# One block for the four upper levels of a recurrence's score matrix, and four residual sums moved to accumulating transfers

## The chip, the cores and the metric

The program runs on one core of one Trainium2 chip. The metric is the device time of one launch in microseconds (us). The kernel before takes 2004.77 us, the median of three runs that lie between 2004.34 and 2007.78 us.

## What is computed

A network of two layers on 1024 tokens of width 1024, all in float32: layer 0 mixes tokens by a sliding-window attention, layer 1 by a gated recurrence of eight heads, and each layer ends with an MLP. The change touches the recurrence alone. Cut to that:

```
def chunk_step(state, inp):            # one chunk of 64 tokens, all heads
    qc, kc, vc, lc = inp               # lc: log of the forget gate
    b = cumsum(lc, axis=2)
    o_inter = einsum('bhtd,bhde->bhte', qc * exp(b), state)
    diff = b[:, :, :, None, :] - b[:, :, None, :, :]
    decay = exp(where(causal, diff, -inf))
    scores = einsum('bhtd,bhtsd,bhsd->bhts', qc, decay, kc)
    o_intra = einsum('bhts,bhse->bhte', scores, vc)
    new_state = exp(b_last) * state + einsum('bhsd,bhse->bhde', kc * exp(b_last - b), vc)
    return new_state, o_inter + o_intra
...
o = rmsnorm(o, g_norm) * silu(g)
x = x + o @ w_o                        # the residual sum after the projection
```

## The kernel before, in words

Activations lie transposed, 128 channels on the partitions and 512 tokens (one half, `hf`) on the free axis. Every large product is a Strassen scheme of matmuls of 128x128 on 512 columns, each made of three (`wh` times high part, `wh` times low part, `wl` times high part), so that a row of three such matmuls is the unit in which TensorE's work is seen.

`Schedule` sets the order. Every operation is recorded with the engines that may run it and a planned cost; a list scheduler runs through them several times, hands out buffers, and writes each engine's instructions in the order that it found. Nothing is reordered on the chip: each engine, and SyncE's queue of transfers, takes its instructions in that order, and waits where an operand is late. All operations are issued by one helper line, so that every row of the profile carries L438; buffers are told apart by their pool: `p` and `q` are PSUM banks (four each), `t` (18 buffers), `a` (60) and `m` (6) are tiles of 128x512 in SBUF, `wr`, `wh` and `wl` hold weights, `d` is DRAM.

In `recurrence`, one call for each head `e`, the decayed scores inside a chunk are found by levels. At each level `double(H, ...)` multiplies half of the elements of `q` and half of those of `k` by the running products of forget gates (`tot`), and matmuls on 32 columns of the array (16 to 64 columns of data each) form the scores between neighbouring blocks of H tokens. `double` works in place, or, with a third argument such as `self.t`, writes new tiles from that pool: then the untouched half is copied by ScalarE. A group of such narrow matmuls is a visit (`visit`): it takes one bank of `q`, and each matmul of the group is made to wait for all operands of the group (`late`), so that the group stands in one piece between the wide matmuls. Before the change a head has four visits: level 0 (64 matmuls of 48 columns), levels 1 and 2 (128 of 16), levels 3 and 4 (128 of 16), and the two upper levels, 5 and 6 (32 of 32 columns and 32 of 64). `merge` copies the scores of a level into the tile `scores` under a mask on VectorE. The gates of the next head, wide matmuls, are laid between the pieces of a head's recurrence (`interleave`); the last head has the first products of the projection beside it.

`hgrn_out` is that projection, seven products in the order 1, 5, 2, 6, 3, 7, 4. After each of the last ones `scaled_sum(hf, m, z)` scales four PSUM banks on VectorE, loads the old residual, and adds. What comes out of the last product, 4, is `x[4..7][0]`; `begin` of the second MLP scales these (`gained`, ScalarE), splits them into high and low parts (ScalarE, then VectorE), and `pair_first` multiplies them into the banks that its rows call `p`. `dma_add` is a transfer issued by GpSimd that adds its source to its destination; it stands in other places of the kernel already.

Of the kernel before, what the change touches and what calls it, by code (L numbers as in the profile page):

```python
# [15 lines left out]
ALU = mybir.AluOpType  # L16
# [137 lines left out]
HK = KT // 2  # L154
# [229 lines left out]
class Net:  # L384
# [1347 lines left out]
    def recurrence(self, e, gates, totals, out):  # L1732
# [5 lines left out]
        tots, tot = [self.t(tag="m") for _ in range(NH)], [g[1] for g in gates]  # L1738
        qs, ks = ([g[i] for g in gates] for i in (0, 2))
        later = lambda z, H: z.rearrange("p (n a h) -> p n a h", a=2, h=H)[:, :, 1]  # L1740
        at = 0

        def level(lg, bank, at, qs, ks, late):
            n = NC * QB // 2
            part = bank[:, at * n : at * n + n].rearrange("p (c t) -> p c t", c=NC)
            for hf, (q, k) in enumerate(zip(qs, ks)):
                for j in range(4 * BPH):
                    rows = slice(j % 4 * QB, j % 4 * QB + QB)
                    self.mm(part[rows, hf * BPH + j // 4], block(k, j), later(block(q, j), 1 << lg), True, True, QB, 1.28, "columns", late)
            return part  # L1750

        def merge(lg, part):
            H = 1 << lg
            n = QB // (2 * H)
            mask = later(self.level_mask[lg], H).unsqueeze(1).to_broadcast([P, NC, n, H])
            target = scores.rearrange("p c (n a h) -> p c n a h", a=2, h=H)[:, :, :, 1]
            part = part if lg == 0 else part.rearrange("p c (n h) -> p c n h", n=n)
            self.op("DVE", nc.vector.copy_predicated, [target], [mask, part], 70 + NC * QB // 2 * 1.04, target, mask, part)

        def visit(operands):  # L1760
            return sum((q + k for q, k in operands), []), self.psum("q")

        for q, f, k, g, v in gates:
            for z, c in zip(q, PAIR):
                z = self.fours(z)
                self.tt("any", z[:, :, ::3].only("f"), z[:, :, 1:3].only("q"), self.pairs(f[:, c]), ALU.mult, TH // 2)
        yield
        late, bank = visit([(sum(qs, []), ks)])
# [10 lines left out]
        at, tot, q1, k1 = self.first_double(qs, ks, tot, tots)  # L1779
        yield  # L1780
        yield
        at, tot, q2, k2 = self.second_double(q1, k1, tot, tots, at)
        yield
        late, bank = visit([(sum(q1, []), k1), (q2, k2)])
# [7 lines left out]
        parts = [part, level(2, bank, 1, q2, k2, late)]  # L1792
        merge(1, parts[0])
        merge(2, parts[1])
        at, tot, qs, ks = self.double(4, q2, k2, tot, tots, at)
        yield
        yield
        at, tot, q4, k4 = self.double(8, qs, ks, tot, tots, at, self.t)
        yield
        late, bank = visit([(qs, ks), (q4, k4)])  # L1800
        parts = [level(3, bank, 0, qs, ks, late), level(4, bank, 1, q4, k4, late)]
        merge(3, parts[0])
        merge(4, parts[1])
        at, tot, q5, k5 = self.double(16, q4, k4, tot, tots, at)
        yield
        yield
        at, tot, q6, k6 = self.double(32, q5, k5, tot, tots, at, self.t)
        yield
        late, bank = visit([(q5, k5), (q6, k6)])
        top = bank[:, : NC * QB // 2].rearrange("p (c t) -> p c t", t=QB)  # L1810
        cross = bank[:, TH // 2 :].rearrange("p (c t) -> p c t", t=CH)
        for hf, (q, k) in enumerate(zip(q5, k5)):
# [3 lines left out]
        for hf, (q, k) in enumerate(zip(q6, k6)):  # L1816
            for j in range(2 * BPH):
                c, r = j // 2, (j // 2 % 2 * 2 + j % 2) * QB
                self.mm(cross[r : r + QB, (hf * BPH + c) // 2], block(k, 4 * c + j % 2), block(q, 4 * c + 2, 2), True, True, CH, 1.05,
                        "columns", late)  # L1820
        qs, ks = q6, k6
        yield
        weights = []
# [12 lines left out]
        at, tot, qs, ks = self.double(CH, qs, ks, tot, tots, at)  # L1836
# [4 lines left out]
        for hf, (q, k) in enumerate(zip(qs, ks)):  # L1841
            v, g = back[2 * hf : 2 * hf + 2]
# [149 lines left out]
    def hgrn_out(self, x, totals):  # L1992

        kept, y, r = {}, {}, [self.a() for _ in range(NH)]
        order = [(name, p) for name in ORDER for p in range(HK)]
        ready = {}

        def operand(name, p):
            w = self.out_weight(name, p, kept)
            z = x[name][p]  # L2000
            return w, self.take_back(z) if isinstance(z, list) else z

        def products(name, bank, start, apart=False):
            todo = order.index((name, 0))
            for p in range(HK):
                for q in order[: todo + p + 1 + AHEAD]:
                    if q not in ready:
                        ready[q] = operand(*q)
            got = [ready[name, p] for p in range(HK)]
            turns = [(p, m) for p in range(HK) for m in range(HK)]  # L2010
            more = {} if start else {"skip_group_check": True}
            for p, m in sorted(turns, key=lambda k: k[1]) if apart else turns:
                c, (w, z) = slice(m * P, m * P + P), got[p]
                self.mm3(bank[m], (w[0][:, c], w[1][:, c]), z, start and p == 0, p == HK - 1, **more)

        def scaled_sum(hf, m, z):
            u, out = self.t(tag="m"), self.a()
            self.tt("DVE", u, z, r[hf], ALU.mult)
            self.dma(out, self.x[m][hf], 4 * P * TH)
            self.tt("any", out, u, out, ALU.add)  # L2020
            self.x[m][hf] = out

        for hf in range(NH):
            self.copy(r[hf], self.rstd(totals[hf], 0.25, 0.25))
        main, side = [self.psum() for _ in range(HK)], [self.psum("q") for _ in range(HK)]
        p1, p5 = ([self.a() for _ in range(HK)] for _ in range(2))
        products(1, main, True)
        for m in range(HK):
            self.copy(p1[m], main[m])
        products(5, main, False)  # L2030
        for m in range(HK):
            w, z = ready[2, 0]
            self.mm(side[m], w[0][:, :P], z[0], True, True)
            self.copy(side[m], p1[m], psum=False)
            self.tt("DVE", p5[m], main[m], p1[m], ALU.subtract)
        products(2, side, False)
        for m in range(HK):
            scaled_sum(0, m, side[m])
        yield
        products(6, main, False)  # L2040
        for m in range(HK):
            self.copy(side[m], main[m])
        products(3, side, False)
        for m in range(HK):
            scaled_sum(1, m, side[m])
        products(7, main, False)
        for m in range(HK):
            self.tt("DVE", side[m], main[m], p5[m], ALU.subtract)
            scaled_sum(1, m + HK, main[m])
        products(4, side, False)  # L2050
        for m in range(HK):
            scaled_sum(0, m + HK, side[m])
        yield
# [153 lines left out]
```

## Time and profile before

| what | value |
|---|---|
| median of the runs | 2004.77 us |
| the profiled execution: its time | 2005.34 us |
| its span, first to last instruction | 2003.4 us |
| TensorE busy | 1992.5 us (99%) |
| VectorE busy | 1810.6 us (90%) |
| ScalarE busy | 1314.1 us (66%) |
| GpSimd busy | 88.3 us (4%) |
| granted TensorE clock, mean | 0.999 |

The time of the profiled execution is 1.9 us longer than its span, and 0.57 us above the median of the three runs. The eight heads lie between about 946 and 1325 us of the span, the projection ends at about 1385 us, and the second MLP follows without a break.

### The profile page before, as it was taken

How to read it: one execution, taken by the hardware profiler on the slowest of the kernel's cores; microseconds unless marked ns; L12 is line 12 of the kernel's file. 1: busy time of each engine (PE TensorE's matmuls, PEld its weight loads, DVE VectorE, ACT ScalarE, POOL GpSimd, SP SyncE). 2: the span in 40 equal slices, each digit the busy share in tenths (PEclk: the TensorE clock that was granted, in tenths of full speed). 3: DMA queues.
4: the chain of work that ended last, by engine and by line, in shares of the span. 5: the costliest groups of instructions: out<-in, count | busy, mean ns of one | idle time of the engine just before them, and what ended most of it. 6: DMA issues, size and time to landing. Idle time of an engine off the chain costs nothing.

```text
span 2003.4 us, 40001 instructions
## 1 busy us (share of the span) xinstructions
PE 1992.5 (99%) x13772; PEld 1692.1 (84%) x13772; DVE 1810.6 (90%) x3669; ACT 1314.1 (66%) x2783; POOL 88.3 (4%) x163
## 2 busy tenths in 40 slices
PE   9999999999999999999999999999999999999998
PEld 8888778899998888888888888888889998888887
DVE  8878999999998979889999999999999998887985
ACT  7777968776674544657666666676867667544573
POOL 2000210000001000000000000000000001100000
PEclk9999999999999999999999999999999999999999
DMA  7848988898899967665888889989788889986812
GB/s 251 258 152 246 259 224 279 289 304 285 272 291 336 332 218 250 218 205 191 280 285 281 291 287 318 319 303 314 252 292 300 264 290 294 341 301 218 272 53 85
DMA packets 293467, 525.97 MB, mean 263 GB/s; under 512 B 33936, under 2 KB 42512, under 8 KB 293264
## 3 DMA queue, kind: packets, MB, share of 16 engines
q1 hardware_dynamic: 283616, 506.09, 74.4%
q0 software_dynamic: 9504, 17.31, 4.9%
q8 instruction: 109, 1.79, 0.4%
q14 instruction: 94, 0.77, 0.1%
q10 hardware_dynamic: 144, 0.02, 0.0%
HBM read 408.89 MB, written 110.72 MB: 259 GB/s over the span
## 4 chain that ended last, share of the span: by engine, by line
PE 92%; DVE 3%; DMA 2%; issue 1%; ACT 1%; POOL 0%; SPq 0%; DVEq 0%; POOLq 0%; ACTq 0%
PE p L438 49%; PE q L438 43%; DVE t L438 2%; DMA d<-t 1%; ACT t L438 1%; DMA a<-in_x 1%; DVE m L438 0%; DVE wl L438 0%; DVE a L438 0%; ACT m L438 0%; DMA a<-a 0%; POOL a L438 0%; DMA a<-d 0%; DMA t<-d 0%; ACT a L438 0%
## 5 line engine op out<-in xcount | busy, mean ns | idle before, releaser
L438 PE MATMUL p<-a,wh 128*128 128x512 f32 (+1 forms) x3056 | 849.6, 363 | 0.1
L438 PE MATMUL q<-a,wh 128*128 128x512 f32 x2084 | 645.7, 391 | 0.0
L438 PEld LDWEIGHTS p<-a,wh 128*128 128x128 f32 x3056 | 542.9, 189 | 86.4 <-DVE a L438 0.9
L438 PE MATMUL p<-a,wl 128*128 128x512 f32 (+1 forms) x1528 | 548.1, 361 | 0.4 <-DVE wl L438 0.4
L438 PEld LDWEIGHTS q<-a,wh 128*128 128x128 f32 x2084 | 387.0, 188 | 77.5 <-DVE a L438 0.7
L438 PE MATMUL q<-a,wl 128*128 128x512 f32 x1040 | 403.8, 390 | 0.0
L438 PEld LDWEIGHTS p<-a,wl 128*128 128x128 f32 x1528 | 287.4, 189 | 43.3 <-DVE wl L438 1.3
L438 ACT CAST wh<-m 128x512 fp32r<-128x512 f32 (+1 forms) x358 | 214.7, 605 | 159.4 <-PE q L438 88.7
L438 ACT CAST wh<-wr 128x512 fp32r<-128x512 f32 (+1 forms) x304 | 181.1, 602 | 136.4 <-PE p L438 88.1
L438 DVE TENSOR_TENSOR wl<-m,wh 128x512 fp32r<-128x512 f32 (+1 forms) x358 | 237.6, 667 | 29.5 <-ACT wh L438 25.3
L438 DVE TENSOR_TENSOR t<-t,t 128x512 f32<-128x512 f32 (+3 forms) x394 | 223.5, 589 | 12.7 <-DMA t<-d 6.7
L438 DVE TENSOR_TENSOR wl<-wr,wh 128x512 fp32r<-128x512 f32 (+1 forms) x304 | 200.5, 664 | 35.7 <-ACT wh L438 28.7
L438 PEld LDWEIGHTS q<-a,wl 128*128 128x128 f32 x1040 | 195.3, 188 | 40.7 <-DVE wl L438 0.5
L438 ACT ACTIVATE t<-t 128x512 f32<-128x512 f32 (+1 forms) x294 | 184.2, 631 | 53.8 <-DVE t L438 49.4
L438 DVE TENSOR_TENSOR a<-t,a 128x512 fp32r<-128x512 f32 (+1 forms) x261 | 174.0, 684 | 19.6 <-PE q L438 7.8
L438 ACT CAST a<-t 128x512 fp32r<-128x512 f32 x181 | 109.6, 617 | 52.0 <-DMA t<-d 37.5
L438 ACT COPY t<-q 128x512 f32<-128x512 f32 (+2 forms) x254 | 111.8, 442 | 30.7 <-PE q L438 22.2
L438 DVE TENSOR_TENSOR t<-t,p 128x256 f32<-128x256 f32 x288 | 116.0, 414 | 16.7 <-PE p L438 12.6
L438 DVE TENSOR_TENSOR a<-a,a 128x512 fp32r<-128x512 f32 (+2 forms) x157 | 105.4, 679 | 11.1 <-ACT a L438 5.3
L438 ACT CAST a<-a 128x512 fp32r<-128x512 f32 x140 | 85.6, 619 | 43.3 <-DVE a L438 34.0
L438 DVE TENSOR_TENSOR m<-wr,wr 128x512 f32<-128x512 f32 (+1 forms) x152 | 97.3, 642 | 0.4
L438 PE MATMUL p<-t,wh 128*128 128x256 f32 x480 | 91.4, 283 | 0.0
(142 smaller groups left out, 2320.2 us busy)
## 6 DMA issues: line engine op xcount, KB each, us to landing
t<-d SPq DMA_DIRECT2D x588, 256.0 KB
a<-d SPq DMA_DIRECT2D x350, 256.0 KB
d<-t SPq DMA_DIRECT2D x318, 256.0 KB
wr<-in_up SPq DMA_DIRECT2D x172, 256.0 KB
wr<-in_down SPq DMA_DIRECT2D x160, 256.0 KB
wr<-in_win SPq DMA_DIRECT2D x68, 256.0 KB
d<-a SPq DMA_DIRECT2D x64, 256.0 KB
wr<-in_wqkv SPq DMA_DIRECT2D x48, 256.0 KB
```

Of the source, the lines that this page charges most:

```text
L438: fn(*[place(a) for a in args], **{k: place(v) for k, v in kw.items()})
```

## The change

Levels 3 and 4 lose their own visit. Their operands `q3`, `k3`, `q4`, `k4` are kept, so that `double(16)` now writes new tiles of the pool `t` (four more copies on ScalarE for each head) instead of working in place, and `double(32)` writes tiles of the pool `a`. The last visit of a head then holds the four upper levels, in two banks of `q`, and all its matmuls wait for the operands of all four levels. The two merges of levels 3 and 4 follow it. In `scaled_sum` the four sums for `x[4..7][0]` are made by `dma_add` in place of an addition on VectorE.

```
-        late, bank = visit([(qs, ks), (q4, k4)])
-        parts = [level(3, bank, 0, qs, ks, late), level(4, bank, 1, q4, k4, late)]
-        merge(3, parts[0])
-        merge(4, parts[1])
-        at, tot, q5, k5 = self.double(16, q4, k4, tot, tots, at)
+        q3, k3 = qs, ks
+        at, tot, q5, k5 = self.double(16, q4, k4, tot, tots, at, self.t)
         yield
         yield
-        at, tot, q6, k6 = self.double(32, q5, k5, tot, tots, at, self.t)
+        at, tot, q6, k6 = self.double(32, q5, k5, tot, tots, at, self.a)
         yield
-        late, bank = visit([(q5, k5), (q6, k6)])
+        bank, more = self.psum("q"), [v for z in (q3, k3, q4, k4) for v in z]
+        late, low = visit([(q5, k5), (q6, k6)])
+        late = late + more
+        parts = [level(3, low, 0, q3, k3, late), level(4, low, 1, q4, k4, late)]
...
+        merge(3, parts[0])
+        merge(4, parts[1])
...
             self.dma(out, self.x[m][hf], 4 * P * TH)
-            self.tt("any", out, u, out, ALU.add)
+            if hf == 0 and m >= HK:
+                self.dma_add(out, u)
+            else:
+                self.tt("any", out, u, out, ALU.add)
             self.x[m][hf] = out
```

On TensorE, in the first head: before, the visit of levels 3 and 4 stands alone between wide matmuls of the next head's gates.

```order
L438 MATMUL p_12390<-a_11177,wl_12207 128x512
L438 MATMUL q_12421<-t_12151,t_12160 32x16 x16
L438 MATMUL q_12421<-t_12165,t_12173 32x16 x16
L438 MATMUL q_12421<-t_12325,t_12332 32x16 x16
L438 MATMUL q_12421<-t_12346,t_12353 32x16 x16
L438 MATMUL p_12501<-a_11997,wh_12223 128x512
```

In the changed kernel, the same engine and head: that visit is gone from its place, 36 wide matmuls earlier, and its 128 matmuls stand ahead of levels 5 and 6, whose own place among the wide matmuls is the old one.

```order
L438 MATMUL p_12499<-a_11141,wl_12401 128x512
L438 MATMUL q_12530<-t_12150,t_12159 32x16 x16
L438 MATMUL q_12530<-t_12165,t_12173 32x16 x16
L438 MATMUL q_12530<-t_12334,t_12338 32x16 x16
L438 MATMUL q_12530<-t_12345,t_12365 32x16 x16
L438 MATMUL q_12605<-t_12368,t_12390 32x32 x8
L438 MATMUL q_12605<-t_12423,t_12492 32x32 x8
L438 MATMUL q_12605<-a_12430,a_12442 32x64 x8
L438 MATMUL q_12605<-a_12446,a_12505 32x64 x8
L438 MATMUL p_12641<-a_11154,wh_12497 128x512
```

One visit of the last head, that of level 0, is broken in two before the change: on TensorE four wide transposes stand inside it.

```order
L438 MATMUL p_17707<-a_17295,wl_17457 128x512
L438 MATMUL q_17716<-t_17221,t_17670 32x48 x8
L438 MATMUL q_17716<-t_17224,t_17670 32x48 x3
L438 MATMUL q_17732<-c_68,t_17712 128x128 x4
L438 MATMUL q_17716<-t_17224,t_17670 32x48 x5
L438 MATMUL q_17716<-t_17279,t_17704 32x48 x8
L438 MATMUL q_17716<-t_17362,t_17704 32x48 x8
L438 MATMUL p_17766<-a_17295,wh_17450 128x512
```

In the changed kernel it is in one piece.

```order
L438 MATMUL p_17529<-a_17481,wh_17634 128x512
L438 MATMUL q_17814<-t_17225,t_17800 32x48 x8
L438 MATMUL q_17814<-t_17231,t_17800 32x48 x8
L438 MATMUL q_17814<-t_17296,t_17757 32x48 x8
L438 MATMUL q_17814<-t_17300,t_17757 32x48 x8
L438 MATMUL p_17529<-a_17437,wl_17645 128x512
```

Behind the projection's last product TensorE multiplies the second MLP's first operands. Before, the first matmul on a split of `x[4][0]` (into `p_19071`) has 14 wide matmuls between it and the last product (the last five are shown, and that matmul).

```order
L438 MATMUL q_19032<-a_18715,wh_18564 128x512
L438 MATMUL q_19032<-a_18728,wh_18564 128x512
L438 MATMUL q_19032<-a_18715,wl_18581 128x512
L438 MATMUL q_19064<-a_18686,wh_18724 128x512
L438 MATMUL q_19064<-a_18704,wh_18724 128x512
L438 MATMUL p_19071<-a_19059,wh_18577 128x512
```

In the changed kernel 30 wide matmuls stand between them; the first on a split of `x[4][0]` (`a_19169`) writes `p_19181`. Those on the splits of `x[5]`, `x[6]` and `x[7]` begin 39, 48 and 58 places behind the last product.

```order
L438 MATMUL q_19162<-a_18916,wh_18747 128x512
L438 MATMUL q_19162<-a_18941,wh_18747 128x512
L438 MATMUL q_19162<-a_18916,wl_18756 128x512
L438 MATMUL p_19181<-a_19169,wh_18626 128x512
L438 MATMUL p_19185<-a_19169,wh_18809 128x512
L438 MATMUL q_19162<-a_18924,wh_18747 128x512
```

## Rows read from the trace of the kernel before

**Rows 1.** Page: busy time by engine, and TensorE's granted clock in 40 slices.

```profile
PE 1992.5 (99%) x13772; PEld 1692.1 (84%) x13772; DVE 1810.6 (90%) x3669; ACT 1314.1 (66%) x2783; POOL 88.3 (4%) x163
PEclk9999999999999999999999999999999999999999
```

**Rows 2.** Two stretches, one head and the projection's end: engines' busy us, clock, DMA share, GB/s.

```profile
997.00:1047.00 50.00, 50.00 (x611) 41.63 (x611) 45.63 (x107) 32.42 (x79) 1.45 (x7) 1.00 0.83 287
1372.00:1410.00 38.00, 38.00 (x168) 30.98 (x167) 37.71 (x62) 29.86 (x55) 0.00 (x0) 1.00 0.86 297
```

**Rows 3.** TensorE's waits over the span, the longest of six (us, times, longest).

```profile
PE p L438 <- DVE t L438: 1.1, 1, 1.1
```

**Rows 4.** TensorE in order of time, first head's third visit: start, us, operation.

```profile
964.73 0.39 PE L438 MATMUL p<-a,wl 128*128 128x512 f32 x1
965.04 1.38 PE L438 MATMUL q<-t,t 128*32 128x16 f32 x128
966.35 0.73 PE L438 MATMUL p<-a,wh 128*128 128x512 f32 x2
966.92 0.40 PE L438 MATMUL p<-a,wl 128*128 128x512 f32 x1
```

**Rows 5.** TensorE in order of time: a whole and the broken visit, seven transposes.

```profile
1097.03 0.39 PE L438 MATMUL p<-a,wl 128*128 128x512 f32 x1
...
1098.16 0.73 PE L438 MATMUL p<-a,wh 128*128 128x512 f32 x2
...
1293.75 0.40 PE L438 MATMUL p<-a,wl 128*128 128x512 f32 x1
1294.07 0.46 PE L438 MATMUL q<-t,t 128*32 128x48 f32 x22
1294.46 0.66 PE L438 MATMUL q<-c,t 128*128 128x128 f32 x4
1295.05 0.70 PE L438 MATMUL q<-t,t 128*32 128x48 f32 x42
1295.67 0.73 PE L438 MATMUL p<-a,wh 128*128 128x512 f32 x2
...
1316.92 0.98 PE L438 MATMUL q<-c,t 128*128 128x128 f32 x7 [0.45 <-DVE t L438]
```

**Rows 6.** ScalarE's copies of 256 columns during the eight heads: busy us, mean ns, idle before.

```profile
L438 ACT COPY t<-t 128x256 f32<-128x256 f32 x80 | 30.9, 412 | 23.1 <-DVE t L438 16.7 <-PE p L438 5.1 <-DMA d<-t 0.3
```

**Rows 7.** TensorE, VectorE and ScalarE in order of time around the projection's end.

```profile
1376.70 8.32 PE L438 MATMUL q<-a,a 128*128 128x512 f32 x36
1384.86 0.62 PE L438 MATMUL q<-a,wh 128*128 128x512 f32 x2
...
1388.03 0.39 PE L438 MATMUL p<-a,wh 128*128 128x512 f32 x1
...
1383.32 1.88 DVE L438 TENSOR_TENSOR m<-q,a 128x512 f32<-128x512 f32 x3
1385.12 1.28 DVE L438 TENSOR_TENSOR a<-m,a 128x512 f32<-128x512 f32 x2
...
1385.83 1.34 ACT L438 ACTIVATE t<-a,c 128x512 f32<-128x512 f32 x2 [1.72 <-DVE a L438]
1387.08 1.14 ACT L438 ACTIVATE a<-t 128x512 fp32r<-128x512 f32 x2
```

**Rows 8.** The accumulating transfers of GpSimd at 303 to 320 us, then over the span.

```profile
L438 POOL DMA_DIRECT2D t<-d x4: 862/1006/1438, 303.0 to 305.8; - x4
DMA to landing us min/median/max: 6.8/8.3/9.9
...
DMA to landing us min/median/max: 3.3/6.8/10.3
```

**Rows 9.** Page: DMA queues, packets, MB, share of 16 engines' span.

```profile
q1 hardware_dynamic: 283616, 506.09, 74.4%
q0 software_dynamic: 9504, 17.31, 4.9%
```

## The prediction

> **What bounds the kernel now.** I read the page's busy times first: TensorE is busy for 1992.5 us of the span of 2003.4 us, at full granted clock in all 40 slices [rows 1]. Then the waits: of the six places where the trace shows TensorE waiting at all, the longest costs 1.1 us [rows 3]. So a microsecond is won only where TensorE does less or passes its work faster, and any microsecond that it is made to wait is lost. The two stretches of the change say the same. In a middle head TensorE is busy for 50.00 of 50 us, VectorE for 45.63, ScalarE for 32.42; at the projection's end TensorE has 38.00 of 38, VectorE 37.71 [rows 2]. VectorE is nearly full there too, but it is not waited for.
>
> The pace of a wide matmul follows from the last product: 36 starts between 1376.70 and 1384.86, 8.16 us, 0.227 us each [rows 7]. What stands above that pace is what a change of the order can win.
>
> **The merged visits.** The matmuls themselves all stay: as many wide ones, and as many narrow ones with the same columns. What goes is one passage for each of eight heads from wide matmuls to narrow ones and back, and the ninth, the break inside the last head's visit of level 0, which the order of the changed kernel doesn't have. The price of a passage is read in two ways. At its edges: in the first head's third visit the first narrow matmul starts 0.31 us behind the wide one before it (0.227 is the pace), and the two wide ones behind the visit take 0.57 us instead of 0.45 [rows 4], so 0.08 + 0.12 = 0.20 us. What is lost inside, when the array empties behind the last narrow one, isn't in these rows, so that is the lower bound. The broken visit shows a whole passage more: from the last wide matmul ahead to the first behind, 1293.75 to 1295.67, it takes 1.92 us, where the whole one takes 1.13 [rows 5]. Of the 0.79 us of difference the four transposes inside are work: seven take 0.98 us and four 0.66, so 0.11 each, 0.43 in all [rows 5]. That leaves 0.36 us, the upper bound, since transposes on both sides of the gap may have passed worse than wide matmuls would. I take 0.30, nearer to the broken visit, the one place where exactly one passage is added. Nine passages: 2.7 us less (8 x 0.20 = 1.6 to 9 x 0.36 = 3.2).
>
> **What the merged visit adds.** ScalarE gets four copies of 256 columns a head, 32 in all, at 412 ns [rows 6]: 1.65 us a head, where it has 17.6 us free of 50 [rows 2]. VectorE's multiplications are the same in number and width. I cost this at nothing. The cover is TensorE's other work: between the visit of levels 1 and 2 and the last one stand 72 wide matmuls of the next head's gates, 16.3 us, before and after alike. If the cover were gone, the 1.65 us a head would be TensorE's wait (rival below). The merges of levels 3 and 4 move behind the last visit; who waits for them is ScalarE's copying of `scores`, and behind that the head's output matmuls, again with wide matmuls beside them. The tiles `q3` to `k5` hold 12 of the 18 `t` buffers, four more than before, until the last visit; the order keeps the place of that visit in the heads before the last, so I give this nothing either.
>
> **The accumulating transfers.** Four additions on VectorE go, which TensorE didn't wait for; nothing is won. In exchange `x[4..7][0]` comes later. Before, the first scaling ends at about 1384.0 (0.68 us from 1383.32), the sum follows at 1385.12, ScalarE scales from 1385.83 and splits from 1387.08, and TensorE takes the first operand at 1388.03 [rows 7]. With the transfer, it is issued at about 1384.1. The nearest row is the burst of four adds into `t` at 303 us: 6.8 us to landing for the fastest, 9.9 for the slowest, issues spread over 2.8 us [rows 8]. I take 6.8 for the first: landed at 1390.9. One scaling and one split, 0.67 and 0.57 us (halves of 1.34 and 1.14), with about 0.3 us on the way to TensorE (1387.65 to 1388.03) [rows 7], come to 1.6 us: ready at 1392.5. The order of the changed kernel asks for it 30 wide matmuls behind the last product, at 1384.86 + 30 x 0.227 = 1391.7. So TensorE waits 0.8 us. The fourth: issued 1386.9, landed 1396.8, ready 1398.4; asked for 58 matmuls on, at 1398.0, late by less than the first wait has already given. The two between, spaced evenly, land at 1392.9 and 1394.8, are ready 1.6 us later, and are asked for 39 and 48 matmuls on, at 1393.7 and 1395.8: late by 0.8 and 0.6, inside the first wait too. I take 0.9 us. Bounds: nothing, if they land in 3.3 us, the fastest of the 66; and 4.3 us, if the first lands in 10.3, the slowest [rows 8] (ready 1396.0).
>
> Who stands behind these waits: on ScalarE, in order, the casts of the next weights (`wh`), which TensorE wants about 16 us behind the last product; on SyncE's queue the store of `x[4][0]` and then loads of MLP weights into `wr`. Both have several microseconds. The adds also load the transfer engines: 1.49 us of all sixteen for each (4.9% of 2003.4 us over 66), against 0.76 for a plain transfer of that size (74.4% over 1970, at 144 packets each) [rows 9]. Four make 6.0 us where the share is 0.86, so 5.3 of 38 us are free [rows 2]: under 1 us of delay for what follows, inside the upper bound.
>
> **A rule that speaks against it.** In [rows 8] the burst at 303 us issues in 862 to 1438 ns each. The Trainium skill, page "SBUF — State Buffer", section "SBUF: two separate sides", in its box on a trap, says that a transfer issued by GpSimd can starve while VectorE runs an operation that takes the port shared by both, because its descriptors can't be written. It names 620 ns for one alone and about 3100 beside such a copy. An estimate from that page is 2.5 us later for each add, and then a wait of 3.3 us here instead of 0.8, which brings the kernel to 2005.5 us; no run here shows a starved add, and the minimum of 862 ns beside a busy VectorE speaks against it.
>
> **Sum.** 2005.34 - 2.7 + 0.9 = 2003.5 us for the profiled execution; that one is 0.57 us above the median, so 2003.0 us for the median, 0.09% less. About 0.2% (4.0 us) can be told from no change here, so I forecast no change that can be told. The likeliest case's own range is 2001.4 to 2004.4.
>
> **The rivals.**
>
> 1. More is won: 0.36 us a passage, adds in time, and the last head's wait of 0.45 us ahead of its transposes [rows 5] gone: 3.2 + 0.45 = 3.7 less, 2001.1 us. For it: the operands of the last visit no longer wait for level 3 and 4's matmuls before `double(16)` overwrites them. Against it: the landing times.
> 2. The adds land late, starved by VectorE or behind the loads: -2.7 + 4.3, 2006.4 us. For it: the share of 0.86 and VectorE full [rows 2]. Against it: 30 matmuls of distance instead of 14.
> 3. The passages give nothing back, because the merged visit changes its columns (16, 32, 64) and banks inside, and that costs as much: 0.9 more, 2005.7 us. Against it: the visits of 48 and 16 columns run through two banks' halves and several tiles in one piece [rows 4].
> 4. Slower: the last visit waits in each head for the added copies, because ScalarE takes its work in order and the visit waits for all its operands: 8 x 1.65 = 13.2 more, 2004.77 - 1.8 + 13.2 = 2016.2 us. It decides for slower from 0.73 us a head ((4.0 + 1.8) / 8). For it: the 12 held `t` buffers thin out the work of the next gates. Against it: 17.6 us free on ScalarE in each head [rows 2], and copies run beside the multiplications.
>
> **How the numbers follow.** Forecast 0.62, rival 1 0.15, rival 2 0.10, rival 3 0.06, rival 4 0.07. Faster by over 0.2%, below 2000.8, is the far part of rival 1: 0.10. Slower by over 0.2%, above 2008.8, is rival 4 and the tail of rival 2: 0.09. Within: 0.81. The range, 2000.6 to 2006.6, takes in both bounds of the passages and of the adds and leaves out the tail of rival 1 and rival 4.
>
> **What would show it.** Three visits a head, the third with 192 narrow matmuls in one piece; the distance from the first head's first visit to the last head's last shorter by about 2.5 us; four adds landing 6 to 10 us behind their issue; a wait of under 2 us of TensorE ahead of the first `p` matmuls behind the projection. Wrong would be a wait ahead of the third visit in each head, a wait of over 4 us behind the projection, or passages that don't shorten the heads.

## The result and the profile after

The changed kernel takes 2019.57 us (median of six runs, 2019.38 to 2020.61), the kernel before 2005.68 us beside it (six runs, 2004.34 to 2007.78): a ratio of 1.0068, 95% interval 1.0056 to 1.0079. It is slower by 0.7%; the forecast was 2003.0 us and no change, so it was wrong, and the time lies far outside the range. All times are medians, and one run of a later experiment (e8c), 3314 us long at a granted clock of 0.556, is left out of its ratio.

| what | after |
|---|---|
| profiled execution: its time / span | 2020.32 / 2018.3 us |
| TensorE busy | 1995.1 us (99%) |
| VectorE / ScalarE / GpSimd busy | 1809.6 / 1323.9 / 91.8 us |
| granted TensorE clock, mean | 0.996 |

TensorE's work hardly grew (+2.6 us busy), the span grew by 14.9. So the difference is waiting, and the view to read first is that of TensorE's waits (tile waited for, what ended the wait: us in total, times, longest), which stands against [rows 3]:

```profile
PE q L438 <- issue: 8.6, 3, 4.5
PE p L438 <- ACT a L438: 2.4, 2, 2.1
PE q L438 <- DVE a L438: 1.6, 2, 1.2
```

Before, no wait was above 1.1 us. Now three waits of 8.6 us in all are ended by "issue": TensorE waited for nothing that the profile shows, no semaphore, no operand. In order of time they stand inside the merged visits of the second, third and seventh heads; here the second and the seventh (start, us, operation, in brackets the idle time ahead):

```profile
1025.09 1.64 PE L438 MATMUL q<-t,t 128*32 128x16 f32 x159
1028.78 0.22 PE L438 MATMUL q<-t,t 128*32 128x32 f32 x1 [2.04 <-issue]
1028.78 0.63 PE L438 MATMUL q<-a,a 128*32 128x64 f32 x29
...
1280.92 1.60 PE L438 MATMUL q<-t,t 128*32 128x16 f32 x154
1287.02 0.28 PE L438 MATMUL q<-t,t 128*32 128x32 f32 x3 [4.49 <-issue]
```

A visit stops with 159, 184 and 154 of its 192 matmuls done, and the rest, whose operands are awaited together with the first, not begun. The lengths of pauses in the text run from the last start ahead to the first start behind: 2.24, 2.26 and 4.69 us here; the idle time in brackets is some 0.2 us less. The five other merged visits of the same kernel run through in 2.0 to 2.2 us. Ahead of none of the eight does a row show a wait, so the copies (my rival 4) are not it.

Behind two of the three pauses the granted clock is at its lower level. The windows (us, busy time and count of each engine, PEclk, DMA share, GB/s) behind the second and the seventh head's pause, and one after each:

```profile
1029.70:1033.00 3.30, 3.30 (x10) 2.55 (x9) 2.24 (x7) 3.13 (x14) 0.97 (x5) 0.50 0.74 277
1033.10:1036.00 2.90, 2.90 (x14) 2.38 (x13) 0.54 (x1) 2.30 (x7) 0.00 (x0) 1.00 0.28 90
1287.10:1292.40 5.30, 5.30 (x49) 4.16 (x49) 2.71 (x7) 4.70 (x19) 1.42 (x6) 0.50 1.00 355
1292.50:1296.00 3.50, 3.50 (x17) 2.90 (x16) 1.29 (x2) 1.34 (x4) 0.00 (x0) 1.00 0.78 245
```

At 0.50 (1.2 in place of 2.4 GHz) up to half of the 3.3 and 5.3 us is lost, 4.3 us. Behind the third head's pause, with 2.04 us of idle time as well, the clock stays up.

What does TensorE wait for, then? The page lists a DMA queue that I never read in the kernel before, where its row is the same but for the share (queue, kind: packets, MB, share):

```profile
q8 instruction: 109, 1.79, 0.4%
```

109 packets of 1.79 MB in all are 16 KB each; TensorE has 13,772 matmuls and as many weight loads, 253 for each packet (256 with its few other instructions, so 64 bytes each). These are TensorE's own instructions, brought in blocks of 256. Two later kernels with 2048 and 1024 more of them (e4, e5) have 117 and 113 packets, 8 and 4 more. Below, the place of an instruction is its number in the order of the program, matmuls, weight loads and semaphore instructions counted, modulo 256. In the trace every pause falls at place 192 to 194, and one such packet ends inside each pause. For the second head's, the window 1026.0 to 1027.5 us:

```profile
q1 hardware_dynamic: 97, 0.19, 34.4%
q8 instruction: 1, 0.02, 4.8%
```

It runs from 1026.23 to 1027.37 us, and TensorE goes on 1.4 us behind its end. In the seventh head it starts at 1284.56, when TensorE has stood for 2.2 us already, ends at 1285.55, and TensorE goes on 1.47 us later. Until it starts (window 1282.33 to 1284.5) the data queue fills the transfer engines:

```profile
q1 hardware_dynamic: 485, 0.88, 105.8%
```

**Theory (supply).** A visit's instructions run at 5.2 ns each (384 in 2.0 us), wide ones at 113 ns (two in 0.227 us). A block that is asked for in time for wide matmuls comes too late when a long run of narrow ones uses the stored instructions up. The earliest packet of both traces starts when TensorE stands at place 152 of a block, and without it TensorE stops at place 192 of the next: 296 instructions, 33 us of wide matmuls but 1.5 us of narrow ones. A visit of 128 matmuls (256 instructions) can't hold such a stretch by itself; the merged one, of 384, holds it when it begins far enough ahead in a block. **Rivals:** the merged visit waits for something of its own (its operands, its second bank, the copies); or the clock falls first and the pause follows.

### The profile page after: what moved, and what is told of

It reads as the page before. It is cut to its first block, busy times and chain, and to the rows that moved or that the text cites. A ratio compares the mean times of both kernels' runs of the same rounds, so it can differ in the third digit from the quotient of the medians.

```text
span 2018.3 us, 40058 instructions
## 1 busy us (share of the span) xinstructions
PE 1995.1 (99%) x13772; PEld 1694.4 (84%) x13772; DVE 1809.6 (90%) x3665; ACT 1323.9 (66%) x2815; POOL 91.8 (5%) x167
## 3 DMA queue, kind: packets, MB, share of 16 engines
q8 instruction: 109, 1.79, 0.4%
## 4 chain that ended last, share of the span: by engine, by line
PE 92%; DVE 4%; DMA 2%; issue 1%; ACT 1%; SPq 0%; DVEq 0%; POOL 0%; POOLq 0%; ACTq 0%
PE p L438 49%; PE q L438 42%; DVE t L438 1%; DVE m L438 1%; DVE a L438 1%; DVE wl L438 1%; ACT t L438 0%; DMA wr<-in_up 0%; ACT m L438 0%; DMA d<-t 0%; DMA a<-a 0%; DMA a<-m 0%; DMA t<-d 0%; DMA a<-in_x 0%; ACT a L438 0%
## 5 line engine op out<-in xcount | busy, mean ns | idle before, releaser
L438 DVE TENSOR_TENSOR t<-t,t 128x512 f32<-128x512 f32 (+3 forms) x394 | 224.5, 591 | 11.9 <-DMA t<-d 6.3
```

Source lines behind the costliest of these rows:

```text
L438: fn(*[place(a) for a in args], **{k: place(v) for k, v in kw.items()})
```

## The experiments

A useful ruler is the start of the same wide matmul in two traces, found by counting (here all matmuls on the whole array count, transposes too; where the order differs, it is the one of the same number). Ahead of the heads all the kernels have one order, so the first column, -0.9 to +1.6 us, shows how far two executions differ by themselves; each row is one trace. The differences to the trace of before, in us, at the 4,701st (929 us before, ahead of the heads), the 6,601st (1351, behind them), the 7,401st (1513, in the second MLP) and the last of 10,012:

| kernel | ahead of heads | behind heads | in the MLP | last |
|---|---|---|---|---|
| after | +0.8 | +12.0 | +14.8 | +15.0 |
| e1, merge alone | +0.4 | +8.1 | +14.4 | +14.3 |
| e2, adds alone | +1.6 | +1.4 | +3.5 | +3.7 |
| e3, after, shifted by 60 | +0.5 | +9.6 | +11.8 | +12.2 |
| e5, level 3 twice | +1.3 | +22.7 | +22.7 | +22.7 |
| e6, merge in five heads | -0.3 | +0.2 | +3.2 | +3.1 |
| e7, in six, shifted | -0.2 | +2.6 | +7.2 | +7.2 |
| e8, five, later transposes | -0.7 | -2.3 | -1.8 | -0.8 |
| e8b, e8 in another order | +0.2 | -0.2 | +0.5 | +0.5 |
| e8c, four, later transposes | -0.2 | -0.5 | +0.8 | +1.5 |
| e9, e7, later transposes | -0.9 | +0.4 | +3.2 | +4.6 |
| e10, e8, shifted by 144 | +1.2 | +11.9 | +12.4 | +12.5 |

**e1 and e2: the two parts alone.** e1 is the changed kernel with the sums on VectorE again, e2 the kernel before with the four sums by transfer.

```
 # e1, in scaled_sum (e2 is the reverse on the kernel before)
-            if hf == 0 and m >= HK:
-                self.dma_add(out, u)
-            else:
-                self.tt("any", out, u, out, ALU.add)
+            self.tt("any", out, u, out, ALU.add)
```

> The changed kernel with the four residual sums on VectorE again, as before the change. TensorE's instructions of the eight heads stand in the same order and at the same places as in the changed kernel. Theory: the pauses inside the merged visits come from TensorE's instruction supply, so the same three visits (second, third and seventh head) pause again, by 2 to 5 us each, with a lowered clock behind one or two of them: 2016 us, some 11 us above before. Rival: the adds or their load on the transfers cause the slow heads; then this is within 2 us of before, or faster by up to 2.7 us.

> The kernel before with the four accumulating transfers alone, visits unchanged. Theory: they cost what TensorE waits behind the projection in the changed kernel, 2.4 us, and at most 1 us more of late followers: 2008 to 2009 us against 2005.7 of before, no pause inside any visit. Rival: the adds are hidden and the 3 us seen behind the projection in the changed kernel come from its shifted order; then within 0.5 us of before.

Measured: e1 2020.48 us, ratio 1.0073 (1.0058 to 1.0088); e2 2007.80, ratio 1.0011 (1.0002 to 1.0020). The merge alone is as slow as both together, and 4.5 us slower than I expected; e1 pauses in the same three visits (1.83, 2.06 and 4.50 us), e2 in none. The two don't add up: behind the heads e1 loses 6.3 us and the whole change 2.8.

**e3: the changed kernel, its instructions shifted.** Fifteen matmuls of one column ahead of the first warming matmul, 60 instructions; all else is in the same order.

```
+    def padded(self, out, w, x, **kw):
+        for _ in range(PAD):                     # 15
+            self.nc.tensor.matmul(out[:QB, :1], w[:, :QB], x[:, :1], start=True, stop=True)
+        self.nc.tensor.matmul(out, w, x, **kw)
```

> The changed kernel with 60 more TensorE instructions (30 tiny matmuls with their weight loads) at its very start; everything else in the same order. Theory of the instruction supply: TensorE's instructions come in blocks of 256 (109 transfers of 16 KB for 27,904 places of 64 B), and a visit pauses where two ends of a block fall into it, with the first of them well inside; counted from the program, the changed kernel's visits begin at places 181, 130, 80, 30, 236, 188, 139, 244 of a block whose end is at 192. A shift by 60 makes it 241, 190, 140, 90, 40, 248, 199, 48. So the third and the fourth head pause, at the second block's end, and the second and the seventh no longer do: two pauses of 2.2 to 4.7 us in place of three, 2009 to 2016 us. Rival: an operand, a PSUM bank or a semaphore is late: the pauses stay in the second, third and seventh head, time 2019.6 us. Rival: the clock falls first and the pause follows: also unmoved.

Measured: 2016.66 us, ratio 1.0051 (1.0035 to 1.0068), just above the expected range. The pauses left the second and seventh heads and stood in the third and fourth (2.31 and 2.38 us), as the count of places said. Nothing that those visits wait for had changed, so operands, banks and copies fall. The last head's visit, at place 48, ends just ahead of the critical place, and TensorE paused 3.26 us ahead of the seventh matmul behind it, which I had not foreseen. All of e3's waits that are ended by "issue":

```profile
PE q L444 <- issue: 4.3, 2, 2.2
PE p L444 <- issue: 2.9, 1, 2.9
```

e3 also prices the pauses, since it has the order of the changed kernel. From the head's first visit to the next head's, the second head takes 53.42 us in the changed kernel and 50.25 in e3, the seventh 55.03 and 48.49: 3.2 and 6.5 us for the pause and the low clock behind it. That is less than 2.24 + 1.65 and 4.69 + 2.65, in part because the pause covers a wait for VectorE that e3 shows in both heads (0.3 us each).

**e4: bursts without any operand.** The kernel before, with runs of 64, 192, 384 and 384 narrow matmuls on constant tiles ahead of products of the MLPs.

```
+BURSTS = {(1, 8): 32, (1, 10): 96, (1, 12): 192, (0, 12): 192}   # (layer, m): float32 matmuls, two each in the trace
+                self.nc.tensor.matmul(out[r : r + QB, :16], z[:, r : r + QB], z[:, :16], start=True, stop=True)
```

> The kernel before with bursts of tiny matmuls of 32 columns on a constant tile, ahead of the first matmul of four products of the two MLPs; they wait for nothing, and the product that follows overwrites what they write. Bursts of 384 (first MLP), 64, 192 and 384 matmuls (second MLP), which with their weight loads are 768, 128, 384 and 768 instructions. Theory of the instruction supply: the burst of 64 runs through, that of 192 pauses once, 253 or fewer places before its end, those of 384 pause twice each, each pause 2 us or more and at a block's end. Rival (operands, banks, semaphores of the recurrence): none of the bursts pauses, they cost about 10 ns a matmul, 10 us in all: 2016 us. With the pauses 10 to 20 us more.

Measured: 2038.79 us (one run). The run of 64 passed; that of 192 paused once (4.51 us), those of 384 twice each (2.89 and 3.20, 3.85 and 2.88), always at place 193 or 194. The first of the two runs of 384:

```profile
511.00 1.89 PE L514 MATMUL q<-c 128*32 128x16 f32 x202
515.59 1.26 PE L514 MATMUL q<-c 128*32 128x16 f32 x128 [2.71 <-issue]
519.86 0.94 PE L514 MATMUL q<-c 128*32 128x16 f32 x54 [3.02 <-issue]
```

The clock stood at 1.00 until the first pause of each of these three runs had begun, and then at 0.50 for 6.8 us (from 516.94 us in the run shown): the clock follows the pause, it does not cause it.

**e5: the visits of before, with as many matmuls as the merged one.** Each matmul of level 3 is issued twice, operands and order stay.

```
+        if self.twice:                            # 32 at the visit of levels 3 and 4
+            fn, self.twice = self.issued_twice, self.twice - 1
```

> The kernel before, with each of the 32 matmuls of level 3 in the visit of levels 3 and 4 issued twice with the same operands, so that this visit of every head is a run of 192 narrow matmuls in the trace (384 instructions) as the merged one is; visits, tiles, banks, copies and VectorE's work stay those of before. By count of TensorE's instructions the visit starts at places 108, 185, 8, 87, 166, 247, 72 and 86 of a block of 256. Supply theory: pauses of 2 to 5 us, at place 192 to 194, in the first, fourth, seventh and eighth heads, at most a short one in the fifth, none in the second, third and sixth; the added matmuls are 64 in each head at about 10.4 ns, 0.67 us, 5.3 us in all; with four pauses of 2.3 us or more and some microseconds of half clock behind them the time is 2019 to 2031 us. Rival (the pause comes from what the merged visit waits for: its four levels' tiles, its second bank, the copies): no pause, 2011 us.

Measured: 2026.99 us, ratio 1.0095 (1.0080 to 1.0111). Pauses in exactly the four named heads, none in the others; the eighth head paused twice (1.90 and 3.27 us), the first time 54 matmuls into its visit, 3.6 us behind the end of the visit before. The second head's visit (place 185) and the fourth's (place 87); L511 issues the doubled matmuls:

```profile
1020.70 1.39 PE L511 MATMUL q<-t,t 128*32 128x16 f32 x127
1021.93 0.18 PE L439 MATMUL q<-t,t 128*32 128x16 f32 x1
1021.94 0.18 PE L511 MATMUL q<-t,t 128*32 128x16 f32 x1
1021.94 0.73 PE L439 MATMUL q<-t,t 128*32 128x16 f32 x63
...
1123.54 0.66 PE L439 MATMUL q<-t,t 128*32 128x16 f32 x51
1126.81 0.30 PE L439 MATMUL q<-t,t 128*32 128x16 f32 x12 [2.60 <-issue]
```

The same visit, with the same operands, passes in one head and stops in the other. And since the order of before is kept, the differences behind the heads stay as they are to the end (+22.7 three times): the loss behind the heads in the other kernels is not a matter of the pauses.

**e6 and e7: merging only where no pause is due.** e6 merges in the first, fourth, fifth, sixth and eighth heads; e7, shifted by 48 instructions, in all but the third and fourth. Sums on VectorE in both.

```
+        if e not in MERGED:                       # e6: (0, 3, 4, 5, 7), e7: (0, 1, 4, 5, 6, 7)
+            late, low = visit([(q3, k3), (q4, k4)])
...
```

> The merged visit in the first, fourth, fifth, sixth and eighth heads alone, the two visits of before in the second, third and seventh; sums on VectorE. The merged visits start at places 181, 32, 238, 190 and 3 of a block. Supply theory: no pause in any of them, clock full, and each merged head gives back a passage of about 0.3 us (the last one two): 2003.6 to 2004.4 us, 1.2 to 2 us less than before. Rival (a merged visit costs something by itself in each head): slower than before by five eighths of the 14.9 us of the merge alone, 2014 us.

> Twelve matmuls of one column (48 instructions) ahead of the first warming matmul, the merged visit in all heads but the third and fourth, sums on VectorE. The merged visits start at places 229, 178, 30, 238, 189 and 38 of a block; the second and seventh heads, which paused in the changed kernel, are among them. Supply theory: no pause in a visit, six or seven passages less: 2003.3 to 2004.1 us. Rival (the second and seventh heads pause for something of their own): pauses of 2 us in the second and of 4 us in the seventh, 2010 us or more.

Measured: e6 2009.63 us, ratio 1.0017 (1.0008 to 1.0026); e7 2011.77, ratio 1.0023 (1.0013 to 1.0032). No visit paused and e6's clock stayed up, as the theory has it, but the gain of 1.2 to 2 us did not come: here my theory was not enough. (e7 paused once, 2.43 us, ahead of the twelfth matmul behind the last head's visit, which began at place 38.) Two more losses show. In the heads e6 gained nothing (-0.3 to +0.2), because something stands behind the merged visit; its fourth head:

```profile
1126.01 0.73 PE L439 MATMUL p<-a,wh 128*128 128x512 f32 x2
1126.58 0.39 PE L439 MATMUL p<-a,wl 128*128 128x512 f32 x1
1127.28 0.44 PE L439 MATMUL q<-c,a 128*128 128x128 f32 x2 [0.31 <-DVE a L439]
1127.56 1.22 PE L439 MATMUL p<-a,wh 128*128 128x512 f32 x4
```

Three wide matmuls behind the visit the new order has two transposes of the tiles that `double(CH)` writes, where before 24 wide ones stood between. VectorE does the two moved merges first:

```profile
1126.28 0.62 DVE L439 COPY_PREDICATED t<-c,q 128x128 f32<-128x128 int32 x2
1126.81 1.43 DVE L439 TENSOR_TENSOR a<-a,m 128x256 f32<-128x256 f32 x4
```

So TensorE waits (0.31 us here, 1.1 in the worst head), and passes to the transposes and back once more. All such waits of e6:

```profile
PE q L439 <- DVE a L439: 3.1, 5, 1.1
```

And behind the heads e6 loses 3.0 us, with the change's own parts nowhere near.

**e8, e8b, e8c, e9: the transposes later.** In the merged heads the planner counts the head's weight tile among what the transposes need; they then stand 28 wide matmuls behind the visit (12 in the last head; the sixth head had 28 before).

```
-                self.transpose(pk[:, c * P : c * P + P], k[:, c * P : c * P + P])
+                self.transpose(pk[...], k[...], weights[:1] if e in MERGED else ())   # e8b: weights
```

> Merged visits in the same five heads as in the kernel that merged five, but in them the planner is told that the first transposes behind the visit need the head's weight tile, so that they stand 28 wide matmuls behind the visit (12 in the last head) and not 3 or 4. Theory: in the kernel with five merged heads the passages were saved (0.36 us each by the edges of the visit without a wait) and given back by the wait of these transposes for VectorE's multiplications behind its two merges (0.5 to 1.3 us a head). Then the waits behind the visits go, a merged head takes 49.5 to 49.7 us from its first visit to the next head's where a head with two visits takes 49.9, and TensorE enters the projection 1.5 to 2 us earlier than before. What follows there is open: by the theory that VectorE has no reserve there and any new order of the program costs 2 to 3 us, the whole is 2004.5 to 2007.5 us; if the projection keeps its time, 2003.5 to 2004.5. Rival (a merged visit costs by itself): the merged heads stay at 50.2 to 50.5 us, 2009 us.

> As the one before, but the transposes are planned behind both weight tiles of the head; the order within the heads is the same but for the last one, and the order around the projection is another. Theory: heads as there; a difference between the two in the stretch from 1340 to 1450 us, by up to 3 us, from the order of VectorE's work there alone.

> As the first, with the last head's visits left as before: four merged heads. Theory: four passages less, 1.2 to 1.5 us earlier at the projection; the order around the projection is again another: 2004 to 2008 us.

> Twelve matmuls of one column ahead of the warming ones and merged visits in six heads, at places 229, 178, 29, 235, 188 and 41 of a block of 256, as in the kernel shifted so, with the transposes 28 wide matmuls behind the visit. Theory: no pause in or behind a visit (the last head's is near the limit: its block end is reached 12 wide matmuls behind the visit), no wait for the transposes, 1.8 to 2.3 us earlier at the projection than before: 2003 to 2007 us, by what the projection's new order costs. Rival: 2011 us as without the later transposes.

Measured: e8 2005.68 us, ratio 1.0001 (0.9993 to 1.0010); e8b 2006.48, 1.0002 (0.9993 to 1.0011); e8c 2006.36, 1.0003 (0.9994 to 1.0012); e9 2007.31, 1.0009 (1.0000 to 1.0018). Against the kernel before, run beside each, the ratio falls from 1.0017 to 1.0001 (e6 to e8) and from 1.0023 to 1.0009 (e7 to e9), some 3 us; in the traces 2.1 and 1.5 us arise in the heads (table) and the rest behind them. The wait for VectorE is gone from e8's rows; a wait of 0.27 us for ScalarE stands nearby in the fourth head:

```profile
1124.28 0.74 PE L439 MATMUL p<-a,wh 128*128 128x512 f32 x2
1124.86 0.40 PE L439 MATMUL p<-a,wl 128*128 128x512 f32 x1
1125.10 0.40 PE L439 MATMUL p<-a,wh 128*128 128x512 f32 x1
1125.77 1.22 PE L439 MATMUL p<-a,wh 128*128 128x512 f32 x4 [0.27 <-ACT t L439]
```

In part this missed: e8's fourth head took 50.2 us from visit to visit, not 49.7; only its first head became shorter by a full microsecond. e8b differs from e8 in the heads (by 1.2 us) and not, as expected, behind them (0.2); e8b and e8c win 0.4 and 0.2 us in the heads, not 1.2 or more. e9 paused 2.27 us behind the last head's visit (place 41), which its expectation called near the limit.

**e10: e8, shifted into the pauses.** The kernel that is level with the one before, and 36 matmuls of one column (144 instructions) at its start.

> The kernel with five merged heads and later transposes, which took the time of the kernel before (ratio 1.0001), with one change: 36 matmuls of one column (144 instructions) ahead of the first warming matmul. All else keeps its order. The merged visits now start at places 69, 176, 126, 79 and 123 of a block of 256. Supply theory: pauses of 2 to 5 us at place 192 to 194 in the first, fifth, sixth and eighth heads, none in the fourth (176); with the half clock that followed most such pauses before (1.7 to 3.4 us lost) the kernel takes 9 to 25 us longer than without the shift: 2015 to 2030 us. Rival (the pauses of the other kernels came from their order of work): 2006 us.

Measured: 2021.95 us, ratio 1.0088 (1.0074 to 1.0102), 16 us more than e8. The fifth head's visit in e8 (place 238) and in e10 (place 126):

```profile
1172.39 1.61 PE L439 MATMUL q<-t,t 128*32 128x16 f32 x157
1173.83 0.22 PE L439 MATMUL q<-a,a 128*32 128x64 f32 x1
1173.83 0.21 PE L439 MATMUL q<-t,t 128*32 128x32 f32 x3
1173.86 0.63 PE L439 MATMUL q<-a,a 128*32 128x64 f32 x31
```

```profile
PE q L445 <- issue: 12.0, 6, 4.2
...
1176.01 1.61 PE L445 MATMUL q<-t,t 128*32 128x16 f32 x157
1177.45 0.22 PE L445 MATMUL q<-a,a 128*32 128x64 f32 x1
1177.45 0.21 PE L445 MATMUL q<-t,t 128*32 128x32 f32 x3
1179.94 0.65 PE L445 MATMUL q<-a,a 128*32 128x64 f32 x31 [2.27 <-issue]
```

The four named heads paused and the fourth did not. The other two of the six waits (1.76 and 0.47 us) stand in visits of 128, which I had not foreseen. Of the 156 visits of 128 in all the traces only these two and one in e8c (0.62 us) stopped for more than 0.4 us, all three at place 193 or 194. They began 249, 235 and 182 instructions ahead of it; why these stopped and others like them did not stays open.

Over the changed kernel and all experiments but e4, 68 visits of 192 matmuls were run. The 16 that began at places 69 to 140 of a block all paused inside (1.8 to 4.7 us); the 52 that began at 3 to 48 or at 166 to 248 did not, though three of these, at 38, 41 and 48, were followed by a pause within 12 matmuls. In the 16 a block's end lies 309 or more instructions into the visit, in the 52 none lies beyond 283; starts between these places were not run.

## Why the prediction was wrong

- **The step that failed** is "What the merged visit adds ... I cost this at nothing. The cover is TensorE's other work". I looked for what the visit waits for, and no other work covers a wait for TensorE's own instructions; the sum priced 192 narrow matmuls in one run as it priced 128 and 64 apart. The pauses (2.24, 2.26 and 4.69 us, 9.2 in all) and the half clock behind them (up to 4.3) cost 11.2 us of the 15.0 net: 3.2 and 6.5 in the second and seventh heads (e3), and by an estimate 1.5 in the third, which takes 51.81 us where the fourth, without a pause, takes 50.36. e3, e4, e5 and e10 show the cause; e10 against e8 prices it at 16 us for six pauses.
- **The price of a passage was right, and it didn't help.** Edges of 0.318, 0.113 and 0.335 us around e6's visits of levels 3 and 4 (starts of the last wide matmul ahead, the first and last narrow one, and the first two wide ones behind), less two paces of 0.227, make 0.31 us; the 192 matmuls take 1.88 us in one piece (e6's fourth head) and 1.15 + 0.73 in two. I had taken 0.30. The last of the prediction's signs of being wrong is what came: the passages didn't shorten the heads.
- **"The merges of levels 3 and 4 move behind the last visit; ... again with wide matmuls beside them"** failed too: in most heads three wide matmuls, not 24, stand ahead of the transposes that wait for VectorE behind these merges. That was to be read from the order of the changed kernel. In e6 it cost the whole gain; e8 got 2 us back in the heads.
- **The accumulating transfers** were mis-sized, and not by their landing. I took 0.9 us, within 0 to 4.3; the changed kernel waits 2.4 us there (row above). The four adds landed in 4.7 to 9.1 us. Not the first operand but the fourth is late most. ScalarE's and TensorE's rows there:

```profile
1410.45 0.63 ACT L438 ACTIVATE t<-a 128x512 f32<-128x512 f32 x1 [2.56 <-DMA d<-t]
...
1411.46 0.72 ACT L438 ACTIVATE t<-a,c 128x512 f32<-128x512 f32 x1
```

```profile
1412.89 0.74 PE L438 MATMUL p<-a,wh 128*128 128x512 f32 x2 [2.09 <-ACT a L438]
```

ScalarE stood idle for 2.56 us until a `t` tile was stored, and the fourth scaling is queued behind that instruction; its add had landed at 1407.34. My sum had no term for ScalarE's queue there. In e2 TensorE waits 1.3 us for ScalarE there, so part of this comes with the adds alone; whether their load on the transfers delays the store, no run tests. The starved issue of the Trainium skill's page "SBUF — State Buffer" (section "SBUF: two separate sides") did not show: the issues took 0.90 to 1.73 us each, those of [rows 8] 0.86 to 1.44, and not 2.5 us more.
- **"Nothing" for everything behind the heads** had no step of its own in my sum. Each kernel whose operations differ is planned anew as a whole, and between the 6,601st and the 7,401st wide matmul the new orders lose 0.5 to 6.3 us, even e6, which changes nothing there; e5, with the order of before, loses 0.0. In the changed kernel this is 2.8 us, and the 2.4 us of the accumulating transfers lie within it. That VectorE, 37.71 of 38 us busy there [rows 2], has no reserve for a worse order is my reading of it; no run tests it alone.
- **The rivals.** The fourth had the right sign and place, waits inside the heads, and the wrong mechanism; that its 2016.2 us comes near is luck.

By the ruler, 11.2 us arise in the heads, 2.8 between them and the 7,401st wide matmul, 0.8 ahead of the heads, where the order is that of before, and 0.2 at the end: 15.0 in all. The three pauses with their low clock account for the 11.2 alone, so the nine passages, 2.8 us by their price, won nothing net, as in e6. What used them up is in part the waits for VectorE that the transposes brought; I can't divide the rest further. No version beat the kernel before; e8 is level with it.

## What to carry to other kernels

Count instructions as well as microseconds: a run of tiny matmuls uses up its instructions some twenty times as fast as wide ones do, and a run that nearly always passes at 256 may stop at 384, depending on where in its block it begins. Read the instruction queue's row before making a burst longer, and if a wait is ended by "issue", look at the places where it falls in the stream of instructions. And where a planner sets the whole order, look in the new order at what moves close behind the changed piece, since a shorter burst can bring its readers too near.

## What the runs showed of the hardware

TensorE's instructions come in packets of 16 KB. In the pauses of the changed kernel a packet took 1.0 to 1.1 us, and TensorE went on 1.4 to 1.5 us behind its end. In the four pauses of over 4 us (changed kernel, e1, e4, e10) the packet started only 2.0 to 2.2 us into the pause, at a DMA share of 1.03 to 1.05; that the data queue delays it is not shown, for at 1.04 two packets of e5 started after 0.5 and 0.9 us. The Trainium skill, page "Runtime: NRT & Kernel Launch", section "Instruction fetch mechanics", says that the sequencer refills in 16 KiB blocks of 256 instructions, which the runs bear out, and that crossing a block is "mostly hidden"; for runs of narrow matmuls the 16 pauses of 1.8 to 4.7 us differ, and the measurement decides. The granted clock halved in some pauses or up to 1.5 us behind them, for 3.4 or 6.8 us: at two of three in the changed kernel, one of three in e1, two of three in e3, in all three runs that paused in e4, in three of four heads in e5, at the only one in e7 and in e9, and at one place in e10, its 4.4 us pause. Why not at the others stays open, as does where exactly in a block the next one is asked for.
